# Moving the differential values ahead of the inverse's corner products in a fused two-block transformer kernel

## The chip, the cores and the metric

The kernel runs on one core of a Trainium2 chip. The metric is the time of one execution on the device in microseconds (us). Each core has five engines with queues of their own: TensorE (PE, matrix products), VectorE (DVE), ScalarE (ACT), GpSimd (POOL) and SyncE (SP, which here issues the loads of weights). An engine takes its instructions in the order of its queue; an instruction whose input is late holds up everything behind it.

## The reference

Two transformer blocks on 512 tokens of width 1024, all in float32. The first block (two layers with attention and a gated feed-forward) is untouched here. In the second block the input goes through one projection into two mixers: an RWKV-7 recurrence with 8 heads of 64, and a differential attention with 4 heads:

```python
def step(state, inp):                      # RWKV-7, per token
    sa = einsum('bhvk,bhk->bhv', state, -kk_t)
    state = state * w_t + sa x (kk_t * a_t) + v_t x k_t      # outer products
    return state, einsum('bhvk,bhk->bhv', state, r_t)
...
attn = softmax(q1 k1) - lam * softmax(q2 k2)    # differential attention
out = einsum('bhqk,bhkv->bhqv', attn, vh)
```

Both outputs are normed, joined and multiplied with w_out; a convolutional feed-forward follows.

## The kernel before

Everything is kept transposed (features on partitions, 512 tokens along the free axis). A product in float32 accuracy is made of three passes: a weight chunk of 128x1024 is loaded by SP into `raw` (three buffers), ACT casts it to `whi` (L178), DVE or POOL subtracts to get the rest, `wlo` (L179), and PE adds hi*hi, hi*lo and lo*hi. `whi` and `wlo` have two buffers each, so the cast of a chunk waits until PE is through with the chunk before the last.

The recurrence is computed in chunks of 64 tokens (8 chunks `c`). Inside a chunk it needs the inverse of a triangular matrix for every head. `within` makes these matrices on PE (`pslm`, masked by DVE into `lms`) and copies their 32x32 blocks into `G`; `inverse32` inverts all blocks on DVE alone (tiles Lb, Xb, Pb, Qb, L1685 to L1707), in one long chain that ends with the transposed results `tN` and `tT`. Two sets of small PE products, the corner products `psi` (L1476, 32x32 pieces, from `tN`) and `psi2` (L1482, from `tT`; the trace calls both tiles psi), build the 64x64 inverses in `TT`. Then the chunk loop runs (L1487 to L1526): per chunk the products pxy, pu, pst and the state `S2`.

The differential attention needs its queries and keys (`diff_qk`, i = 0 to 7, tile psd) and its values (`diff_v`, two halves of two weight chunks; 96 matrix products of 256 columns each, tile psdv, L1317, copied to `dv` by ACT, L1322). `work` is the generator of its 16 query blocks: a step is a pair of scores (PE z, DVE L680, ACT L682), a turn (`t`, L698) or a product with the values (`o`, L706); it has 50 steps. `fill(n)` runs n steps of a generator between the products of the recurrence.

The order around the change: two blocks set the order of PE by hand (`manual_schedule` for PE). The first ends with `diff_qk(4..7)` and `diff_v(0)`, the second begins with the corner products. The second half of the values, `values1 = diff_v(1)`, is a generator with 8 pieces of 12 products; VF = (3, 2, 2, 2) spreads it: three pieces between `psi` and `psi2`, two after `chunk_in(0)`, two inside chunk 0, the last in `rest()`. Only then may `work` begin, as it uses the xl tiles as scratch. The later fills are FILLS = (2, 2, 1, 6, 6, ...): 2, 2 and 1 steps per chunk, and 6 and 6 in `tail`, which is placed by the planner. The other engines' queues are ordered by the planner, a simulation with costs of its own: it puts first what it expects to be ready first. `zero` (L1385, POOL) shares its buffer with `Qb` of the inverse. The copies from tT to TT go to DVE (L1463) and ACT (L1464). SLOTS says which part of the recurrence runs where between the `diff_qk`.

Of the kernel before, what the change touches and what calls it, by code (L numbers as in the profile page):

```python
# [12 lines left out]
ALU = mybir.AluOpType  # L13
# [13 lines left out]
def f(t):  # L27
    return t.bitcast(F32)
# [54 lines left out]
class Net:  # L83
# [88 lines left out]
    def chunk(self, ap, eng=None, raw=None, parts=None):  # L172
        nc, n = self.nc, ap.shape[-1]
        if raw is None:
            raw = self.wp.tile([128, 1024], F32, tag="raw", name="raw", bufs=3)
            nc.sync.dma_start(out=raw[:, :n], in_=ap)
        hi, lo = parts or [self.wp.tile([128, 1024], F32R, tag=n_, name=n_, bufs=2) for n_ in ("whi", "wlo")]
        nc.scalar.copy(out=hi[:, :n], in_=raw[:, :n])  # L178
        (eng or nc.vector).tensor_sub(out=lo[:, :n], in0=raw[:, :n], in1=f(hi[:, :n]))  # L179
        return hi, lo  # L180

# [930 lines left out]
    def block2_attn(self):  # L1112
        nc, A = self.nc, self.A
        v_, g_, s_, t_ = nc.vector, nc.gpsimd, nc.scalar, nc.tensor
        with ExitStack() as st:
# [224 lines left out]
            with self.tc.manual_schedule(engines={mybir.EngineType.PE}):  # L1340
# [3 lines left out]
                for ks in (range(7), (7,)):  # L1344
                    for ps, (hi, lo) in zip(first, ws):
                        for k in ks:
                            c = slice(k * 128, k * 128 + 128)
# [25 lines left out]
                X, tN, tT = self.inverse32(pp, G)  # L1373
                dv = pp.tile([128, 4, 512], F32, tag="dv", name="dv")
                for i in range(4, 8):
                    diff_qk(i, g_)
                list(diff_v(0))
            values1 = diff_v(1)
# [3 lines left out]
            xs2, uv2, bv2, y2 = [pp.tile([128, 1056], F32, tag=f"bk{i}", name=n_)[:, 0:1024].rearrange("p (a b) -> p a b", a=2) for i, n_ in enumerate(("xs", "uv", "bv", "yy"))]  # L1382
            yv = lambda t, c: t[:, c % 2, :].rearrange("p (h v) -> p h v", v=64)
            zero = pp.tile([128, S], F32R, tag="zq", name="zero")
            g_.tensor_scalar(out=zero.rearrange("p (a b) -> p a b", a=4), in0=self.ident.unsqueeze(1).to_broadcast([128, 4, 128]),  # L1385
                             scalar1=0.0, scalar2=None, op0=ALU.mult)
            dist2 = [pp.tile([128, S], F32, tag="smask", name="dist"), None]
            nc.sync.dma_start(out=dist2[0], in_=A["dist"])
            S2, yr = [], []
# [2 lines left out]
            def rest():  # L1392
                for _ in values1:
                    pass
                dist2[1] = self.xp.tile([128, S], F32, tag="xh2", name="dist2")
                yr.extend(self.xp.tile([128, S], F32, tag=f"xh{4 + t}", name=f"yr{t}") for t in range(4))
                for i in range(2):
                    S2.append(self.xp.tile([128, 4, 2, 64], F32, tag=f"xh{i}", name=f"S{i}"))
                    g_.memset(S2[i], 0.0)
# [13 lines left out]
            fill = lambda n, of=work: [next(of, None) for _ in range(n)]  # L1413
# [33 lines left out]
            def tail():  # L1447
                chunk_out(7)
                fill(FILLS[3])
                norm_out(2)  # L1450
                fill(FILLS[4])
                norm_out(3)
                fill(1000)

            with self.tc.manual_schedule(engines={mybir.EngineType.PE}):

                TT = [pp.tile([128, 4, 2, 64], F32, tag=n_, name="TT") for n_ in ("pb0", "pb1", "e20", "e21")]
                pm = pp.tile([128, 4, 8, 32], F32, tag="bk2", name="pm")
                half = [(64 - 64 * par, slice(64 - 64 * par, 96 - 64 * par), slice(96 - 64 * par, 128 - 64 * par)) for par in range(2)]
                for t in range(4):  # L1460
                    for _, lo, hi in half:
                        g_.memset(TT[t][hi, :, :, 0:32], 0.0)
                        v_.tensor_copy(out=TT[t][lo, :, :, 0:32], in_=tT[lo, :, 2 * t:2 * t + 2, :])  # L1463
                        s_.copy(out=TT[t][hi, :, :, 32:64], in_=tT[hi, :, 2 * t:2 * t + 2, :])  # L1464

                def corner(ps, hh, rows, mm, out):
                    for par in range(2):
                        for cp in range(4):
                            for h in range(4):
                                mm(ps[half[par][rows], cp, h, :], par, cp, 4 * hh + h)  # L1470
                    for par in range(2):
                        out(par, ps[half[par][rows]])

                for hh in range(2):
                    ps = ((pg, pv)[hh]).tile([128, 4, 4, 32], F32, tag="go"[hh], name="psi")
                    corner(ps, hh, 2, lambda o, par, cp, h: t_.matmul(o, lm(par, cp, h)[half[par][1], half[par][0] + 32:half[par][0] + 64],  # L1476
                                                                      tN[half[par][1], cp, h, :], start=True, stop=True),
                           lambda par, p: (s_.copy if par else v_.tensor_copy)(out=pm[half[par][2], :, 4 * hh:4 * hh + 4, :], in_=p))
                fill(VF[0], values1)
                for hh in range(2):  # L1480
                    ps = pc.tile([128, 4, 4, 32], F32, tag="c", name="psi2")
                    corner(ps, hh, 1, lambda o, par, cp, h: t_.matmul(o, pm[half[par][2], cp, h, :], tT[half[par][2], cp, h, :], start=True, stop=True),  # L1482
                           lambda par, p: [(s_.copy if par else v_.tensor_copy)(out=TT[2 * hh + i][half[par][1], :, :, 32:64], in_=p[:, :, 2 * i:2 * i + 2, :])
                                           for i in range(2)])
                chunk_in(0)
                fill(VF[1], values1)
                for c in range(8):  # L1487
                    cp, par = c // 2, c % 2
                    U = E[1 - par]
                    b, uv, xs = banks[c], uv2[:, c % 2, :], xs2[:, c % 2, :]  # L1490
                    if c:
                        for t in range(4):
                            t_.matmul(b[:, t * 128:t * 128 + 128], ar[t][:, c, :], S2[c % 2][:, t].rearrange("p e v -> p (e v)"),
                                      start=False, stop=True, skip_group_check=True)
                    v_.tensor_copy(out=xs[U, 0:256], in_=b[U, 0:256])
                    v_.tensor_copy(out=xs[U, 256:512], in_=b[U, 256:512])
                    if c:
                        chunk_out(c - 1)
                    fill(FILLS[0]) if c else fill(VF[2], values1)
                    for g in range(2):  # L1500
                        pu = pc.tile([128, 256], F32, tag="c", name="pu")
                        for h in range(4 * g, 4 * g + 4):
                            t_.matmul(pu[U, hs[h - 4 * g]], TT[h // 2][U, cp, h % 2, :], xs[U, hs[h]], start=True, stop=True)
                        (s_.copy if g else v_.tensor_copy)(out=uv[U, 256 * g:256 * g + 256], in_=pu[U])
                    if c:
                        fill(FILLS[1])
                    else:
                        rest()
                        fill(VF[3])
                    if c < 7:  # L1510
                        ps = pc.tile([128, 4, 64], F32, tag="c", name="pst")
                        for h in range(8):
                            t_.matmul(ps[E[h % 2], h // 2, :], bkt[:, c, hs[h]], uv[:, hs[h]], start=True, stop=True)
                        for e in range(2):
                            new = S2[(c + 1) % 2][E[e], :, e, :]
                            if c == 0:
                                v_.tensor_copy(out=new, in_=ps[E[e]])
                            else:
                                old = S2[c % 2][E[e], :, e, :]
                                g_.tensor_tensor(out=new, in0=old, in1=dcs[E[e], :, c:c + 1].to_broadcast([64, 4, 64]), op=ALU.mult)  # L1520
                                v_.tensor_tensor(out=new, in0=new, in1=ps[E[e]], op=ALU.add)
                    if c < 7:
                        chunk_in(c + 1)
                    fill(FILLS[2])
                    if c in (4, 6):
                        norm_out(c // 2 - 2)  # L1526
                if TAIL[0] == 0:
                    tail()
# [320 lines left out]
FILLS = (0, 2, 2, 4, 6)  # L1849
# [139 lines left out]
def constants():  # L1989
# [37 lines left out]
VF = (3, 2, 2, 2)  # L2027
# [18 lines left out]
FILLS = (2, 2, 1, 6, 6, 0, 0)  # L2046
# [2 lines left out]

SLOTS = [["", "", "", "", "decays", "norm1 next keep:01"],  # L2050
         ["late keep:2", "turn:v keep:3", "keep:4", "within:0 within:1 norm1 keep:5", "turn:bh bonus keep:6", "turn:kh within:2 within:3 next keep:7"],
         ["late", "turn:v", "", "within:0 within:1", "within:2 within:3 bonus", "turn:bh turn:kh"]]
CUT = (5, 5)
NEWT = 1
FAST = (0, 0, 0, 1)
# [24 lines left out]
```

## Time and profile before

| | us |
|---|---|
| median of 3 runs | 2021.73 (2016.67 to 2022.11) |
| profiled execution, its own time | 2025.36 |
| span in that profile (first to last instruction) | 2023.6 |
| PE busy | 1934.1 (96%) |
| DVE busy | 1348.1 (67%) |
| ACT busy | 892.2 (44%) |
| POOL busy | 420.5 (21%) |

Busy times are of the whole span. Matrix products are pipelined, so the duration of one is longer than the distance to the next. PEclk is the granted clock of TensorE, as a share of 2.4 GHz; 0.50 is its lower level, 1.2 GHz. The stretch that the change touches runs from 1408 to about 1590 us of the span.

### The profile page before, as it was taken

The page shows a single profiled execution, that of the slowest core. Times are in us where ns is not written, and L with a number is a line of the kernel's source. Part 1 is how long each engine was busy: PE and PEld are TensorE (multiplying, and loading weights), DVE is VectorE, ACT ScalarE, POOL GpSimd, SP SyncE. Part 2 cuts the span into 40 slices and gives each one's busy share as a digit, 9 for nine tenths or more (in the row PEclk, how much of TensorE's full clock was granted, in tenths as well). Part 3 has the DMA queues.
Part 4 walks back from the last instruction along what each step waited for, and adds up shares of the span by engine and source line. Part 5 has one row for each costly group of instructions (what it writes and reads, how often), then busy time and mean ns, then how long its engine had stood idle before and what let it go on. Part 6 is the DMA issues. An engine that isn't in the chain of part 4 may idle for free.

```text
span 2023.6 us, 29687 instructions
## 1 busy us (share of the span) xinstructions
PE 1934.1 (96%) x11652; PEld 1655.3 (82%) x11652; DVE 1348.1 (67%) x2295; ACT 892.2 (44%) x1530; POOL 420.5 (21%) x429
## 2 busy tenths in 40 slices
PE   9999998999999999988999999899899999999997
PEld 8766788999997877778899998678687788888886
DVE  6555568777777576557868676777948568666424
ACT  5454444444444555444434344544245445444321
POOL 3434210000002175320000001344333242111001
PEclk9998998999999999999999999999989999999999
DMA  4210142423223210123423232322111113232332
GB/s 162 99 58 7 32 155 84 138 71 118 88 82 100 74 49 23 32 81 121 142 77 111 87 107 61 111 97 69 63 43 34 63 55 103 95 103 94 95 95 71
DMA packets 58124, 169.58 MB, mean 84 GB/s; under 512 B 6304, under 2 KB 13504, under 8 KB 57984
## 3 DMA queue, kind: packets, MB, share of 16 engines
q1 hardware_dynamic: 54672, 162.70, 24.5%
q10 hardware_dynamic: 3232, 4.72, 0.7%
q8 instruction: 92, 1.51, 0.3%
q14 instruction: 48, 0.39, 0.1%
q0 software_dynamic: 80, 0.26, 0.1%
HBM read 161.89 MB, written 5.77 MB: 83 GB/s over the span
## 4 chain that ended last, share of the span: by engine, by line
PE 80%; DVE 13%; ACT 3%; issue 2%; DMA 1%; POOL 1%; SPq 0%; DVEq 0%; ACTq 0%; POOLq 0%
PE pa L733 8%; PE o L185 7%; PE o L184 6%; PE o L186 6%; PE pb L733 5%; PE p L733 4%; PE pd L186 4%; PE pd L184 4%; PE pd L185 4%; PE po L706 2%; PE t L698 1%; DVE l L217 1%; PE psq L184 1%; PE psq L185 1%; PE psq L186 1%
## 5 line engine op out<-in xcount | busy, mean ns | idle before, releaser
L178 ACT CAST whi<-raw 128x1024 fp32r<-128x1024 f32 (+3 forms) x146 | 144.5, 992 | 273.3 <-PE o L185 91.0
L179 DVE TENSOR_TENSOR wlo<-raw,whi 128x1024 fp32r<-128x1024 f32 (+3 forms) x138 | 164.1, 1190 | 123.0 <-ACT whi L178 122.7
L733 PE MATMUL pa<-t,h 128*128 128x256 f32 x960 | 177.7, 286 | 10.1 <-DVE u L910 8.4
L1044 POOL TENSOR_TENSOR acc<-acc,sqt 128x256 f32<-128x256 f32 (+1 forms) x58 | 70.8, 1220 | 489.7 <-ACT sqt L1043 488.2
L217 DVE TENSOR_TENSOR l<-r,h 128x1024 fp32r<-128x1024 f32 x104 | 127.1, 1222 | 56.1 <-ACT h L216 55.8
L733 PEld LDWEIGHTS pa<-t,h 128*128 128x128 f32 x960 | 152.5, 194 | 12.1 <-ACT ah L861 8.7
L733 PE MATMUL pa<-t,l 128*128 128x256 f32 x480 | 137.5, 286 | 2.2 <-DVE l L217 2.2
L216 ACT CAST h<-r 128x1024 fp32r<-128x1024 f32 x104 | 107.9, 1046 | 65.2 <-PE pd L185 19.9
L185 PE MATMUL o<-xl,whi 128*128 128x512 f32 (+1 forms) x352 | 134.6, 382 | 2.1 <-DVE xl L224 2.1
L184 PE MATMUL o<-xh,whi 128*128 128x512 f32 (+1 forms) x352 | 134.8, 383 | 0.0
L186 PE MATMUL o<-xh,wlo 128*128 128x512 f32 (+1 forms) x352 | 134.0, 381 | 0.0
L186 PE MATMUL pd<-ah,l 128*128 128x512 f32 x320 | 125.6, 392 | 1.9 <-DVE l L217 1.9
L184 PE MATMUL pd<-ah,h 128*128 128x512 f32 x320 | 125.6, 392 | 0.3 <-ACT h L216 0.3
L185 PE MATMUL pd<-al,h 128*128 128x512 f32 x320 | 125.3, 391 | 0.0
L733 PE MATMUL p<-t,h 128*128 128x256 f32 x640 | 116.8, 283 | 4.2 <-ACT h L216 4.2
L733 PE MATMUL pb<-t,h 128*128 128x256 f32 x640 | 116.5, 282 | 0.0
L733 PEld LDWEIGHTS p<-t,h 128*128 128x128 f32 x640 | 99.9, 190 | 5.9 <-ACT h L216 4.6
L733 PEld LDWEIGHTS pb<-t,h 128*128 128x128 f32 x640 | 99.9, 191 | 0.9
L216 ACT CAST h<-raw 128x768 fp32r<-128x768 f32 (+2 forms) x76 | 62.4, 821 | 82.3 <-PE pd L185 58.8
L733 PEld LDWEIGHTS pa<-t,l 128*128 128x128 f32 x480 | 93.1, 194 | 3.0 <-DVE l L217 3.0
L733 PE MATMUL p<-t,l 128*128 128x256 f32 x320 | 90.6, 283 | 3.0 <-DVE l L217 3.0
L733 PE MATMUL pb<-t,l 128*128 128x256 f32 x320 | 90.6, 283 | 1.0 <-DVE l L217 1.0
(550 smaller groups left out, 5338.1 us busy)
## 6 DMA issues: line engine op xcount, KB each, us to landing
r<-w_gu SPq DMA_DIRECT2D x88, 512.0 KB, 3.5
raw<-w_gu SPq DMA_DIRECT2D x56, 512.0 KB, 3.4
raw<-w_dn SPq DMA_DIRECT2D x48, 384.0 KB, 4.1
raw<-w_in SPq DMA_DIRECT2D x22, 512.0 KB, 3.4
raw<-w_dn SPq DMA_DIRECT2D x16, 448.0 KB, 3.2
raw<-w_qka SPq DMA_DIRECT2D x8, 512.0 KB, 3.5
raw<-w_dn SPq DMA_DIRECT2D x16, 256.0 KB, 2.6
raw<-w_out SPq DMA_DIRECT2D x8, 512.0 KB, 3.4
```

Of the source, the lines that this page charges most:

```text
L178: nc.scalar.copy(out=hi[:, :n], in_=raw[:, :n])
L179: (eng or nc.vector).tensor_sub(out=lo[:, :n], in0=raw[:, :n], in1=f(hi[:, :n]))
L184: mm(out, lh, rh, start=start, stop=False)
L185: mm(out, lh, rl, start=False, stop=False)
L186: return mm(out, ll, rh, start=False, stop=stop)
L216: self.nc.scalar.copy(out=hi, in_=src)
L217: (eng or self.nc.vector).tensor_sub(out=lo, in0=src, in1=f(hi))
L698: nc.tensor.transpose(t[:, c], s[:, c], self.ident)
L706: nc.tensor.matmul(po[:, b * 128:b * 128 + 128], v(kb), w[:, kb * 128:kb * 128 + 128], start=kb == 0, stop=kb == b)
L733: self.nc.tensor.matmul(c, l, r, start=first and n == 0, stop=k == 3 and n == 2, skip_group_check=True)
L1044: return nc.gpsimd.tensor_add(out=self.acc[:, c], in0=self.acc[:, c], in1=t)
```

## The change

All pieces of `values1` are now run by `rest()` at the head of the second block, ahead of the corner products; `zero` is made after that and pinned behind what is already traced on POOL; the ACT copies into TT are put behind the last weight cast of the values in ACT's queue. The places that were filled with pieces of `values1` are filled with as many steps of `work`. In SLOTS, the last two `within` move up beside the first two, ahead of the first half of `diff_qk(2)` instead of into its middle.

```diff
-        nc.scalar.copy(out=hi[:, :n], in_=raw[:, :n])
+        self.cast = nc.scalar.copy(out=hi[:, :n], in_=raw[:, :n]).ins
...
-            g_.tensor_scalar(out=zero.rearrange("p (a b) -> p a b", a=4), in0=self.ident.unsqueeze(1).to_broadcast([128, 4, 128]),
-                             scalar1=0.0, scalar2=None, op0=ALU.mult)
...
-                for t in range(4):
-                    for _, lo, hi in half:
-                        g_.memset(TT[t][hi, :, :, 0:32], 0.0)
-                        v_.tensor_copy(out=TT[t][lo, :, :, 0:32], in_=tT[lo, :, 2 * t:2 * t + 2, :])
-                        s_.copy(out=TT[t][hi, :, :, 32:64], in_=tT[hi, :, 2 * t:2 * t + 2, :])
+                rest()
+
+                self.tc.keep_in_program_order(g_.tensor_scalar(
+                    out=zero.rearrange("p (a b) -> p a b", a=4), in0=self.ident.unsqueeze(1).to_broadcast([128, 4, 128]),
+                    scalar1=0.0, scalar2=None, op0=ALU.mult))
+                with self.tc.issue_after(self.cast):
+                    for t in range(4):
+                        for _, lo, hi in half:
+                            ... (the same three)
...
-                fill(VF[0], values1)
+                fill(VF[0])
...
-                fill(VF[1], values1)
+                fill(VF[1])
...
-                    fill(FILLS[0]) if c else fill(VF[2], values1)
+                    fill(FILLS[0]) if c else fill(VF[2])
...
-                        rest()
                         fill(VF[3])
...
-         ["late", "turn:v", "", "within:0 within:1", "within:2 within:3 bonus", "turn:bh turn:kh"]]
+         ["late", "turn:v", "", "within:0 within:1 within:2 within:3", "bonus", "turn:bh turn:kh"]]
```

## Rows read from the trace of the kernel before

**Rows 1.** The page: busy time of PE and DVE; the chain that ended last.
```profile
PE 1934.1 (96%) x11652; PEld 1655.3 (82%) x11652; DVE 1348.1 (67%) x2295; ACT 892.2 (44%) x1530; POOL 420.5 (21%) x429
...
PE 80%; DVE 13%; ACT 3%; issue 2%; DMA 1%; POOL 1%; SPq 0%; DVEq 0%; ACTq 0%; POOLq 0%
```

**Rows 2.** PE's waits, 1440 to 1600: total us, times, longest.
```profile
PE psi L1476 <- DVE tN L1706: 9.9, 1, 9.9
PE pu L1503 <- DVE xs L1495: 1.6, 1, 1.6
```

**Rows 3.** Windows: length, busy us (instructions) of each engine, granted clock, DMA.
```profile
1446.20:1452.20 6.00, 6.00 (x50) 5.79 (x48) 5.83 (x10) 1.05 (x1) 0.00 (x0) 1.00 0.22 81
1452.20:1462.40 10.20, 0.29 (x4) 0.08 (x2) 9.99 (x10) 0.00 (x0) 3.67 (x2) 0.75 0.00 0
1462.40:1467.40 5.00, 5.00 (x50) 4.94 (x51) 4.02 (x9) 3.13 (x8) 0.15 (x1) 0.50 0.29 105
1467.40:1474.30 6.90, 6.90 (x126) 6.77 (x125) 0.70 (x1) 5.34 (x10) 3.21 (x2) 0.99 0.24 78
1474.30:1477.70 3.40, 3.40 (x19) 3.36 (x17) 0.70 (x1) 0.58 (x1) 2.07 (x2) 0.51 0.21 60
1477.70:1484.20 6.50, 6.50 (x150) 6.34 (x149) 0.76 (x2) 0.62 (x2) 2.02 (x2) 0.99 0.14 52
1484.20:1491.40 7.20, 7.20 (x43) 6.83 (x40) 2.30 (x5) 1.67 (x3) 2.04 (x2) 0.53 0.01 2
...
1497.40:1556.00 58.60, 57.60 (x624) 45.99 (x623) 50.40 (x184) 34.91 (x93) 22.12 (x24) 1.00 0.03 11
1556.00:1562.90 6.90, 4.62 (x50) 3.82 (x49) 6.76 (x31) 2.50 (x6) 0.00 (x0) 1.00 0.20 61
1562.90:1587.20 24.30, 22.50 (x128) 17.26 (x127) 16.51 (x62) 14.17 (x35) 4.80 (x4) 0.79 0.33 113
```

**Rows 4.** Timeline of POOL: start, length, instruction, idle before it and its releaser.
```profile
1425.57 2.39 POOL L179 TENSOR_TENSOR wlo<-raw,whi 128x1024 fp32r<-128x1024 f32 x1 [3.92 <-ACT whi L178]
...
1458.73 1.49 POOL L1385 TENSOR_SCALAR zero<-ident 128x512 fp32r<-128x512 f32 x1 [13.78 <-DVE Pb L1701]
1460.18 2.37 POOL L179 TENSOR_TENSOR wlo<-raw,whi 128x1024 fp32r<-128x1024 f32 x1
```

**Rows 5.** Timeline of ACT: TT copies, a weight cast, the copies of the first values.
```profile
1464.19 3.30 ACT L1464 COPY TT<-tT 32x256 f32<-32x256 f32 x8 [16.94 <-DVE tT L1707]
1467.51 1.05 ACT L178 CAST whi<-raw 128x1024 fp32r<-128x1024 f32 x1
...
1470.91 1.57 ACT L1322 ACTIVATE dv<-psdv,rsy 128x256 f32<-128x256 f32 x4 [1.21 <-PE psdv L1317]
```

**Rows 6.** Timeline of SP: the four loads of the value weights.
```profile
1427.99 17.32 SPq L176 DMA_DIRECT2D raw<-w_dv  x4
```

**Rows 7.** Timeline of DVE: masks of `within`, and pieces of the inverse.
```profile
1410.97 0.68 DVE L1286 TENSOR_TENSOR lms<-pslm,lmask 128x512 f32<-128x512 f32 x1
1414.39 0.69 DVE L1286 TENSOR_TENSOR lms<-pslm,lmask 128x512 f32<-128x512 f32 x1 [2.73 <-PE pslm L1283]
...
1425.75 2.54 DVE L1689 TENSOR_TENSOR Pb<-Xb,Lb 128x162 f32<-128x162 f32 x1
...
1428.68 0.54 DVE L1689 TENSOR_TENSOR Pb<-Xb,Lb 128x200 f32<-128x200 f32 x1
...
1456.74 1.90 DVE L1701 TENSOR_TENSOR Pb<-Qb,Xb 128x1024 f32<-128x1024 f32 x1
...
1462.19 1.96 DVE L1707 STREAM_TRANSPOSE tT<-Xb 128x1024 f32<-128x1024 f32 x1
```

**Rows 8.** Timeline of PE: the first product after the stall; two steps of work.
```profile
1462.39 1.94 PE L1476 MATMUL psi<-tN,lms 32*32 32x32 f32 x36 [9.91 <-DVE tN L1706]
...
1568.58 1.06 PE L706 MATMUL o<-w,dv 128*128 128x128 f32 x8
1569.56 1.13 PE L679 MATMUL z<-dqk,dqk 64*128 64x512 f32 x4
```

More of the change, by code (lines that the diff above doesn't have):

```diff
@@ L1459, in block2_attn @@
                 half = [(64 - 64 * par, slice(64 - 64 * par, 96 - 64 * par), slice(96 - 64 * par, 128 - 64 * par)) for par in range(2)]
-                for t in range(4):
-                    for _, lo, hi in half:
-                        g_.memset(TT[t][hi, :, :, 0:32], 0.0)
-                        v_.tensor_copy(out=TT[t][lo, :, :, 0:32], in_=tT[lo, :, 2 * t:2 * t + 2, :])
-                        s_.copy(out=TT[t][hi, :, :, 32:64], in_=tT[hi, :, 2 * t:2 * t + 2, :])
+                rest()
[5 more added lines that the diff above has]
+                        for _, lo, hi in half:
+                            g_.memset(TT[t][hi, :, :, 0:32], 0.0)
+                            v_.tensor_copy(out=TT[t][lo, :, :, 0:32], in_=tT[lo, :, 2 * t:2 * t + 2, :])
+                            s_.copy(out=TT[t][hi, :, :, 32:64], in_=tT[hi, :, 2 * t:2 * t + 2, :])
                 def corner(ps, hh, rows, mm, out):
```

## The prediction

> **What bounds the kernel now.** I read the page's busy times first, then the chain that ended last: PE is busy 96% of the span and carries 80% of that chain [rows 1], so a change pays only where PE waits or runs at its lower clock. PE's waits in the stretch of the change are next: one of 9.9 us stands out, the first `psi` waiting for `tN` of the inverse; the next longest in the list is 1.6 us [rows 2]. The windows then give each part of the stretch, and the reader should see two kinds of loss there [rows 3]. From 1452.2 to 1462.4 PE is busy 0.29 of 10.2 us: 9.9 us idle. And in three windows it is busy all the time at a granted clock of about 0.50, which is 1.2 GHz: 5.0 us at 0.50, 3.4 at 0.51, 7.2 at 0.53. Work done there would have taken half the time at 2.4 GHz; length times (1 - clock) gives 2.5 + 1.7 + 3.4 us, and 0.1 from the two windows at 0.99 between: 7.7 us. Together the old order loses 17.6 us between 1452 and 1492.
>
> Why PE idles is read on POOL and ACT. The second weight chunk of the first values needs its `wlo` from POOL. POOL holds `zero` first, which waits 13.78 us for the buffer of `Qb`, that is for DVE's last L1701; `wlo` starts at 1460.18 [rows 4], though its cast, the one ACT instruction (1.05 us) of the window from 1446.2, was over by 1447.3 [rows 3]. So values that have nothing to do with the inverse wait for it. ACT repeats the pattern one step later: the TT copies wait 16.94 us for `tT`, and the cast of the third chunk stands behind them until 1467.51, though its buffer was free when the first chunk was used up at 1452.2 [rows 3, 5].
>
> **The change part by part.** *Values ahead, `zero` pinned behind, TT copies behind the last cast.* The first chunk's 48 products run as before to 1452.2, 0.12 us each (50 in 6.0 us [rows 3]). The second `wlo` follows its cast at 1447.3 and takes 2.4 us [rows 4]; at 1449.7 it is there before PE asks. PE goes on to 1452.2 + 5.8 = 1458.0. The third chunk: cast at 1452.2, 1.05 us [rows 5], `wlo` to 1455.8, asked for at 1458.0. All four loads were issued by 1445.3 [rows 6] and move past nothing. One new wait: half of the second psdv pair is in a single PSUM bank, free only when ACT has copied the first values, 1.57 us after 1458.0 [rows 5]; six products (0.7 us) go ahead of it, and with the hand-overs I take 1.1 us (0.9 to 1.6). What stands behind on PE is the rest of the values, nothing else. The fourth chunk: cast after those copies to 1460.7, `wlo` to 1463.1, asked for at 1464.9. PE ends the values at 1446.2 + 23.0 + 1.1 = 1470.3. On POOL the memsets of S2 and `zero` (1.49 us [rows 4]) come after 1463.1 and are first wanted by the chunk products behind `psi` and `psi2`, some 10 us later; that work hides them. The 9.9 us go whole.
>
> *What is late next.* The inverse must be done by 1470.3. It ended with `tT` at 1464.15 [rows 7]. Three POOL subtractions now fall into it. The trace shows what one does: a Pb product of 162 elements takes 2.54 us while POOL's `wlo` runs, one of 200 elements 0.54 alone [rows 4, 7], so 2.0 us each, 6.0 in all.
>
> *`within` together.* The third mask of `within` came at 1414.39; now it can follow the second at 1411.65 [rows 7], so the inverse starts 2.7 us earlier. PE's work there is the same and only in another order: nothing on PE. `tT` is then at 1464.15 + 6.0 - 2.7 = 1467.5 and `tN` 2 us before, 4.8 us ahead of PE. That is the cover; if it failed by x us, PE would idle x. The TT copies (3.30 us on ACT [rows 5]) end at 1470.8, before anything needs TT.
>
> *Steps of `work` in place of pieces of values.* Seven steps move from the end of the stage to here; PE has the same work in sum. But the pieces of values were good cover: 128-row products with no waits. A score step waits for DVE to empty two PSUM banks. I count three places with new waits: the three scores between `psi` and `psi2`, the copies xs ahead of pu, the copies uv ahead of pst. The loop's own mix of the same steps leaves 1.0 us idle in 58.6 [rows 3], the lower end (near zero a place); the pu wait of 1.6 us [rows 2] at each place, 4.8, the upper. I take 3.0 us, nearer to the upper end, as here scores follow each other directly.
>
> *Clock.* With the values, the dense work between the corner products is gone. In the old order the clock fell once PE had run `psi` (6.9 us at 0.99, then 3.4 at 0.51) and again after `psi2` (6.5 at 0.99, then 7.2 at 0.53) [rows 3], each time without idle. Those two cost 5.1 us. The fall at 1462.4, after the stall, disappears with it. Now the two sets stand near each other and `psi2` may itself run at 1.2 GHz: at worst one unbroken stretch from 1474 to about 1493, 19 us, 9.5 lost. At best none, since the chunk loop's mix of the same steps holds 1.00 for 58.6 us. I take 7 us, midway between 5.1 and 9.5, because what lies between is scores, not dense products.
>
> The Trainium skill, "TensorE: Matmul & The Clock Gate", section "HAM oscillation — how this bites in real kernels", puts it as a matter of gaps: PE loses its clock when it sits idle too long. By that rule the new order, without long gaps, would keep 2.4 GHz, a rival below. The trace speaks against it: PE was busy 6.90 of 6.90 us before the fall to 0.51 [rows 3].
>
> *The tail.* The steps 39 to 45 of `work` leave it: one pair of scores at 1.13 us and some 20 passes of 128 columns at 0.13 (8 in 1.06) [rows 8], about 4 us of PE. From 1556 to 1587.2 PE loses 2.3 + 1.8 us idle and 0.21 of 24.3 = 5.1 us by the clock [rows 3], while the norm of the last chunk goes its way over DVE, POOL and ACT. With fewer scores DVE serves that chain sooner. Ends: 4 us worse, if the chain is as long and PE merely idles, to 4.6 better, if half of the 9.2 lost there goes; I take 1.5 better, a little to the better side of the middle, as DVE is shown busy 16.5 of 24.3 us there.
>
> **Sum.** Gone: 9.9 + 7.7 = 17.6. New: 1.1 + 3.0 + 7.0 = 11.1. Tail: 1.5 better. Gain 8.0 us. The profiled execution took 2025.36 us, 3.6 above the median of the runs; all terms are differences within one stage, so I take them from the median: 2021.73 - 8.0 = 2013.7. What this kernel's measurement can tell from no change is about 0.3%, 6.1 us: the border of faster is 2015.7.
>
> **The rivals.**
> *The clock holds*: no clock loss, 7 us more gain, 2006.7. For it: the loop's mix at 1.00. Against: the two falls without idle. 0.12. It is what the Trainium skill's rule on gaps would lead to.
> *The tail gives it back*: the end of the stage hangs on the last chunk's chain, and the 4 us of steps that filled PE there are missing. Tail 4.0 worse instead of 1.5 better: gain 2.5, 2019.2. For it: PE is idle and half-clocked there already. Against: the products with w_out fill in, and the chain itself waits behind score work on DVE. 0.18.
> *The queue trap moves*: the planner, which expects the inverse early, puts another instruction that waits for the inverse ahead of one that PE needs (the copies of the first values behind the TT copies, say). PE then waits from 1458.7 to about 1467.5 again, 8.8 us, and the change doesn't do what it says: 2022.5. Against: the pins name the two traps seen. 0.09.
> *Slower: the clock stays down in the chunk loop.* Place: PE after `psi`. With no dense product left, the clock that falls at about 1474 isn't given back by the 64-row work. Without clock loss the gain is 15.0 us, so from 30 us at 1.2 GHz on, that is from about 1504, the change loses; to the end of the loop at 1540 it would be 66 us, 33 lost, 18 us slower: 2039.7. For it: the longest stretch at 0.53 was the one with the most small products in it. Against: the loop held 1.00 throughout. 0.06.
> The forecast has 0.55; its own range is 2010 to 2017.5.
>
> **Chances.** Faster by over 0.3%: 0.78 of the forecast (0.43), all of the held clock (0.12), 0.02 of the tail's: 0.57. Slower by over 0.3%: the clock rival 0.06, and 0.03 of the queue trap with other bad placements by the planner: 0.09. Same: the rest, 0.34. The range goes from the held clock to the tail's case and the queue trap's edge, 2006 to 2021; left out is most of the slower case and half the trap.
>
> **What would show it.** In the new profile: `zero` behind the last `wlo` of the values on POOL; 192 psdv products in one row at about 0.12 us with one gap near 1 us, ended by 1470 to 1471; `psi` starting without waiting for `tN`; a DVE chain whose tT ends near 1467; a clock of 0.5 from about 1474 for some 14 us; the chunk loop at 1.00 again; a tail with fewer scores and an earlier last norm. Wrong would be: a wait of `psi` for `tN` of several us (the cover was too thin), a copy or cast on ACT behind TT copies, a clock of 0.5 beyond 1500, or a tail in which PE idles more than the 4.1 us of before.

## The result: slower by 0.5%, and the profile after

The changed kernel takes 2029.7 us (2027.16 to 2032.29), the kernel before 2021.26 us beside it: a ratio of 1.0051, 95% interval 1.0038 to 1.0064. Forecast were 2013.7 us. The page after, busy times and chain, against [rows 1]:

```profile
PE 1937.0 (95%) x11652; PEld 1655.5 (82%) x11652; DVE 1350.9 (67%) x2295; ACT 893.0 (44%) x1530; POOL 419.4 (21%) x429
...
PE 82%; DVE 10%; issue 3%; ACT 3%; DMA 1%; POOL 1%; SPq 0%; DVEq 0%; ACTq 0%; POOLq 0%
```

DVE's share of the chain fell from 13% to 10%, PE's grew from 80% to 82%. Next PE's waits from 1380 to 1620, where [rows 2] had `psi` waiting 9.9 us for `tN`:

```profile
PE psdv L1317 <- ACT whi L178: 10.3, 1, 10.3
PE z L679 <- DVE smst L680: 2.3, 2, 1.9
PE psdv L1317 <- POOL wlo L179: 1.8, 1, 1.8
```

`psi` no longer waits. The values do: 10.3 us for a cast and 1.8 us for the subtraction behind it. ACT shows who held that cast (start, length, instruction, idle before it and its releaser):

```profile
1443.01 1.05 ACT L178 CAST whi<-raw 128x1024 fp32r<-128x1024 f32 x1 [4.39 <-PE psd L185]
1462.78 1.24 ACT L1422 COPY uv<-vt 64x512 f32<-64x512 f32 x2 [18.72 <-DVE tT L1710]
1464.04 1.05 ACT L178 CAST whi<-raw 128x1024 fp32r<-128x1024 f32 x1
1465.12 1.57 ACT L1322 ACTIVATE dv<-psdv,rsy 128x256 f32<-128x256 f32 x4
...
1467.64 3.30 ACT L1468 COPY TT<-tT 32x256 f32<-32x256 f32 x8
```

The TT copies stand behind the last cast, as the change asks. But the two `uv` copies that `chunk_in` issues (L1422) now stand ahead of the third value cast. They write the tile with tag bk1, which the inverse's `Xb` holds until `tT` has read it, so ACT sits idle for 18.72 us. In the kernel before, the same copies came behind that cast, which started at 1467.51 [rows 5]:

```profile
1468.46 1.24 ACT L1424 COPY uv<-vt 64x512 f32<-64x512 f32 x2
```

POOL shows the planned half of the change at work, against [rows 4]: the second `wlo` at 1444.13 follows its cast at once, and `zero` is last:

```profile
1444.13 2.40 POOL L179 TENSOR_TENSOR wlo<-raw,whi 128x1024 fp32r<-128x1024 f32 x1 [2.40 <-ACT whi L178]
1465.17 2.35 POOL L179 TENSOR_TENSOR wlo<-raw,whi 128x1024 fp32r<-128x1024 f32 x1 [18.63 <-ACT whi L178]
...
1473.45 1.50 POOL L1460 TENSOR_SCALAR zero<-ident 128x512 fp32r<-128x512 f32 x1
```

The windows after (columns as in [rows 3]; the first figure after the five engines is the granted clock):

```profile
1442.99:1454.72 11.73, 11.73 (x97) 11.52 (x95) 11.42 (x14) 1.05 (x1) 2.40 (x1) 1.00 0.25 86
1454.72:1467.60 12.88, 0.78 (x4) 0.32 (x2) 10.21 (x14) 4.76 (x8) 2.35 (x1) 0.62 0.00 0
1467.60:1471.30 3.70, 3.70 (x17) 3.70 (x18) 0.00 (x0) 3.23 (x9) 1.16 (x2) 0.50 0.41 142
1471.30:1480.83 9.53, 9.53 (x81) 9.40 (x79) 1.23 (x1) 1.66 (x3) 5.11 (x4) 1.00 0.36 112
1480.83:1485.00 4.17, 4.17 (x133) 4.12 (x132) 0.90 (x2) 2.46 (x5) 0.00 (x0) 1.00 0.02 4
1485.00:1515.60 30.60, 28.34 (x252) 21.92 (x248) 15.20 (x51) 8.46 (x28) 4.76 (x5) 0.50 0.06 18
...
1536.30:1556.00 19.70, 18.70 (x202) 15.02 (x200) 17.36 (x63) 11.89 (x30) 6.98 (x8) 1.00 0.01 2
1556.00:1590.00 34.00, 31.89 (x308) 26.30 (x307) 30.65 (x113) 20.28 (x48) 8.66 (x8) 1.00 0.28 94
```

Two losses show. From 1454.7 to 1467.6 PE is busy 0.78 us: idle as before, for another instruction. And from 1485.0 to 1515.6, after `psi`, it is busy 28.34 of 30.60 us at 0.50, 1.2 GHz; nothing of this length stands in [rows 3]. PE's own timeline shows it in one pair, `psi` and `psi2`, 128 products of 32x32 each in the trace, 3.93 us at 1.00 and 6.47 us at 0.50:

```profile
1480.83 3.93 PE L1480 MATMUL psi<-tN,lms 32*32 32x32 f32 x128
...
1487.14 1.43 PE L679 MATMUL z<-dqk,dqk 64*128 64x256 f32 x4 [1.95 <-DVE smst L680]
...
1491.13 6.47 PE L1486 MATMUL psi<-tT,pm 32*32 32x32 f32 x128
```

To compare kernels I count, over windows of 1 us from 1440 to 1600, PE's idle time (length less busy) and what the clock takes (busy time x (1 - granted clock)). Before: 15.0 idle + 12.5 clock = 27.5 us. After: 18.7 + 19.8 = 38.5. That is 11.0 us more, beside 10.3 us by the ratio. The count takes the clock's loss at its highest: of the 6.47 us of `psi2` it calls 3.2 lost, and the pair above shows 2.5.

### The profile page after: what moved, and what is told of

It is laid out like the page before. It is cut to its first block, busy times and chain, and to the rows that moved or that the text cites. A ratio compares the mean times of both kernels' runs of the same rounds, so it can differ in the third digit from the quotient of the medians.

```text
span 2030.4 us, 29687 instructions
## 1 busy us (share of the span) xinstructions
PE 1937.0 (95%) x11652; PEld 1655.5 (82%) x11652; DVE 1350.9 (67%) x2295; ACT 893.0 (44%) x1530; POOL 419.4 (21%) x429
## 4 chain that ended last, share of the span: by engine, by line
PE 82%; DVE 10%; issue 3%; ACT 3%; DMA 1%; POOL 1%; SPq 0%; DVEq 0%; ACTq 0%; POOLq 0%
PE pa L733 8%; PE o L185 6%; PE o L186 6%; PE o L184 6%; PE pb L733 5%; PE p L733 4%; PE pd L186 4%; PE pd L184 4%; PE pd L185 4%; PE po L706 2%; PE t L698 1%; DVE l L217 1%; PE psq L184 1%; PE psr L184 1%; PE psq L185 1%
## 5 line engine op out<-in xcount | busy, mean ns | idle before, releaser
L733 PE MATMUL pa<-t,h 128*128 128x256 f32 x960 | 177.6, 286 | 10.3 <-DVE u L910 8.4
```

The costliest lines, as they stand in the source:

```text
L733: self.nc.tensor.matmul(c, l, r, start=first and n == 0, stop=k == 3 and n == 2, skip_group_check=True)
```

## Experiments

Theory 1: the queue trap moved to the `uv` copies. Theory 2: with the dense value products gone from between `psi`, `psi2` and chunk 0, the clock falls and stays low, idle or not.

**The uv copies behind the last value cast** (uv_pinned).

```
+                last_cast.append(self.cast)          # behind rest()
...
-                s_.copy(out=uv2[V, c % 2, :], in_=vt[V, cp, :])
+                with self.tc.issue_after(last_cast[0]):
+                    s_.copy(out=uv2[V, c % 2, :], in_=vt[V, cp, :])
```

> The changed kernel with one thing more: the two `uv` copies that `chunk_in` issues on ScalarE (line 1422, the first waits for the inverse's last transpose) are held behind the last cast of the differential values' weights, as the copies of TT already are; nothing else differs. Theory 1 (the trap went to another instruction): these copies, planned ahead of the third value cast, hold it and with it the 64 products of the second half. The waits of 10.3 + 1.8 us go, and the 3.7 us of products at half clock behind them run at full clock (1.9 us): 2029.7 - 14.0 = 2015.7 us. Theory 2 (no dense products left behind psi): a second loss of some 15 us stays, seen as a granted clock of 0.50 for about 30 us while psi2, z, t, o and the first chunk run. Rival A: that half clock is a consequence of the idle 12 us before; then it goes with the stall, and the time is near 2001 us. Rival B: something else holds the third cast (its transfer, a free buffer): the time stays at 2029 to 2030 us and the wait keeps its size under another name.

Measured 2016.58 us (2011.01 to 2018.69), 0.9982 of before (0.9974 to 0.9991). ACT now, with the third value cast at 1447.25, released by PE, the fourth at 1453.69, and the copies behind all casts of the values:

```profile
1447.25 1.05 ACT L178 CAST whi<-raw 128x1024 fp32r<-128x1024 f32 x1 [5.13 <-PE psdv L1317]
...
1453.69 1.05 ACT L178 CAST whi<-raw 128x1024 fp32r<-128x1024 f32 x1
1463.07 3.31 ACT L1471 COPY TT<-tT 32x256 f32<-32x256 f32 x8 [8.33 <-DVE tT L1713]
1466.39 1.25 ACT L1424 COPY uv<-vt 64x512 f32<-64x512 f32 x2
```

Its windows, the values and `psi` first:

```profile
1441.60:1465.36 23.76, 23.28 (x190) 22.59 (x188) 23.25 (x26) 6.30 (x13) 12.89 (x7) 1.00 0.25 84
1465.36:1469.30 3.94, 3.93 (x129) 3.82 (x128) 0.64 (x2) 3.87 (x8) 0.00 (x0) 1.00 0.01 4
1469.30:1489.50 20.20, 17.82 (x167) 12.70 (x168) 11.12 (x34) 7.91 (x23) 2.04 (x2) 0.50 0.16 53
...
1489.50:1513.10 23.60, 21.61 (x240) 17.18 (x241) 15.26 (x52) 11.61 (x32) 8.72 (x10) 0.99 0.01 2
1513.10:1520.30 7.20, 7.20 (x46) 6.55 (x44) 4.26 (x21) 2.60 (x7) 1.56 (x3) 0.55 0.01 2
```

The stall is gone with one pin: theory 1 holds, rival B falls. Rival A falls too: PE was busy 27.2 of 27.7 us when the clock fell at 1469.3, right behind `psi`, and it stayed at 0.50 for 20.2 us. Here the half clock came without a long idle time before it. The Trainium skill ("TensorE: Matmul & The Clock Gate", section "HAM oscillation — how this bites in real kernels") ties the loss to idle gaps; this trace doesn't agree: the 27.7 us before the fall hold 0.5 us of idle time in all.

**`zero` alone pinned, values where they were** (zero_pin_alone).

```
-            g_.tensor_scalar(out=zero..., scalar1=0.0, scalar2=None, op0=ALU.mult)
+            self.tc.keep_in_program_order(g_.tensor_scalar(out=zero..., scalar1=0.0, scalar2=None, op0=ALU.mult))
```

> The kernel before with one edit: `zero` on GpSimd (line 1385) keeps its place in program order, behind the first two wlo of the differential values, so that it cannot be planned ahead of the second wlo; the four pieces of the values stay between the inverse's products as they were. Theory 2 (the dense value products between psi, psi2 and the first chunk keep TensorE's clock up): the wait of 9.9 us goes and no new half clock comes: 2021.3 - 9.9 = 2011.4 us, down to 2003.7 if the half clock before psi goes as well. Rival: the planner finds another instruction to put ahead (a copy that waits for the inverse ahead of a cast), and the wait stays at 9 to 12 us under another name: 2020 to 2024 us.

Measured 2013.38 us (2010.15 to 2015.26), 0.9964 (0.9951 to 0.9977). One added call gives nearly the time that was forecast for the whole change, but not in the way expected: the wait shrinks from 9.9 to 6.2 us only. Counted from the start of `Lb`, PE asks for `psi` 5.6 us later, as it now runs the other 47 products of the first values ahead of it, and `tN` comes 1.9 us later, with one more subtraction beside the inverse:

```profile
PE psi L1477 <- DVE tN L1707: 6.2, 1, 6.2
```

The clock is at 0.50 for the 12.9 us that begin with `psi`, this time behind idle time, and at 0.53 for 3.3 us behind `psi2`. With value pieces in between, it is then 1.00 up to 1556:

```profile
1461.40:1474.30 12.90, 11.12 (x149) 10.85 (x149) 5.29 (x11) 8.95 (x18) 5.18 (x3) 0.50 0.14 42
1474.30:1481.70 7.40, 7.40 (x162) 6.99 (x160) 1.52 (x4) 1.20 (x4) 3.32 (x4) 0.96 0.25 75
1481.70:1485.00 3.30, 3.30 (x18) 3.18 (x17) 0.77 (x2) 0.17 (x2) 0.74 (x1) 0.53 0.00 0
1485.00:1556.00 71.00, 68.36 (x724) 55.69 (x724) 57.53 (x212) 39.39 (x101) 22.11 (x24) 1.00 0.06 17
```

**Values dealt out again, all casts up front** (split_4211), on top of uv_pinned.

```
+                cs = [self.chunk(A["w_dv"][2 * half + c], g_) for c in range(2)] if half else None
...
-                    hi, lo = self.chunk(A["w_dv"][2 * half + c], g_)
+                    hi, lo = cs[c] if half else self.chunk(A["w_dv"][c], g_)
...
-                rest()
+                fill(4, values1)     # ahead of psi
...
-                fill(VF[0])
+                fill(2, values1)     # between psi and psi2
...
-                fill(VF[1])
+                fill(1, values1)     # behind chunk_in(0)
...
+                        rest()       # in chunk 0
                         fill(VF[3])
```

> The kernel of uv_pinned with the eight value pieces dealt out again, behind their casts: four ahead of psi, two between psi and psi2, one behind the first chunk_in and the last inside chunk 0, whose work steps then follow it; all casts are issued before any copy that waits for the inverse. Theory 1 and 2 together: no wait for a cast, and the clock between psi and chunk 1 is 1.00 or falls for less than 15 us: 2029.7 - 14.0 - 10 to 15 = 2000.7 to 2005.7 us. Theory 1 alone (the half clock has nothing to do with where the value products stand): as uv_pinned, near 2015.7 us. Rival A (half clock follows the idle time): as uv_pinned too, both near 2001 us.

Measured 2007.1 us (1997.22 to 2009.71), 0.9927 (0.9909 to 0.9945): the lowest median of the study, and 1.4 us above the range expected. It differs from uv_pinned by where four of the eight pieces stand (both casts of this half come ahead of `psi`, as they do there), and 1.2 GHz shrinks from 20.2 + 7.2 us up to 1556 to 6.4 + 3.2 us:

```profile
1457.40:1461.50 4.10, 2.35 (x75) 2.35 (x75) 4.05 (x4) 0.52 (x2) 3.67 (x4) 0.95 0.41 128
1461.50:1467.90 6.40, 6.40 (x75) 6.34 (x73) 3.68 (x10) 5.55 (x11) 0.00 (x0) 0.50 0.01 3
1467.90:1474.90 7.00, 7.00 (x158) 6.52 (x158) 2.68 (x7) 1.83 (x5) 1.87 (x2) 0.99 0.26 77
1474.90:1478.10 3.20, 3.20 (x22) 2.98 (x22) 0.37 (x2) 0.00 (x0) 0.17 (x1) 0.50 0.00 0
1478.10:1556.00 77.90, 75.14 (x770) 60.03 (x768) 67.86 (x244) 48.16 (x124) 26.72 (x27) 1.00 0.15 49
```

By this alone the order of other work could be the reason as well. Hence the next two.

**Zero products behind psi and psi2** (dense).

```
+                banks[0] = pr.tile([128, 512], F32, tag="r", name="pxy")
+                for _ in range(12):    # once behind psi, once behind psi2
+                    t_.matmul(banks[0], zero[:, 0:128], zero, start=True, stop=False, skip_group_check=True)
```

> The kernel of uv_pinned with work added that changes no value: 24 zero products of 128x512, twelve right behind psi and twelve right behind psi2, into the bank that chunk 0 clears with such a product anyway. At 0.23 us each (two psdv products of 256 columns at 0.12 us) they cost 5.6 us at full clock. Theory 2 (it is the want of dense products behind psi that brings 0.50, and no idle time is needed for it): the 19.6 us at 0.50 behind psi shrink to 8 us or less, which gives back 5.8 us or more: 2012 to 2017 us, against 2016.6 without them. Rival (0.50 comes on its own course, or after the waits of 1.5 us and less in this stretch): the half clock keeps its 20 us, the products cost 5.6 us or, in part at 0.50, up to 8: 2022 to 2025 us.

Measured 2013.17 us (2009.96 to 2015.01), 0.9964 (0.9948 to 0.9980). With 24 products more that change nothing, the kernel is 3.4 us faster than uv_pinned by the medians, 3.6 by the ratios (each run has its own measurement of the kernel before beside it). The two intervals overlap a little, so what is safe is that 5.5 us of added work (24 products at 0.23 us) cost nothing that shows. The single 0.50 of 20.2 us becomes two parts, 0.63 over 4.6 us and 0.55 over 7.2 us:

```profile
1471.40:1476.00 4.60, 4.60 (x14) 3.38 (x16) 3.16 (x4) 2.83 (x6) 0.00 (x0) 0.63 0.49 127
1476.00:1481.20 5.20, 4.50 (x82) 3.25 (x83) 3.90 (x20) 3.28 (x12) 0.00 (x0) 1.00 0.25 94
1481.20:1488.40 7.20, 7.20 (x78) 6.17 (x72) 2.16 (x6) 1.25 (x4) 2.04 (x2) 0.55 0.00 0
```

**The control: small products in place of the zero products** (light): `psi`'s own products again, 64 calls behind `psi` and 64 behind `psi2`, into the same bank.

```
+                t_.matmul(banks[0].rearrange(...)[half[par][2], cp, h, :], lm(par, cp, h)[...],
+                          tN[half[par][1], cp, h, :], start=True, stop=True, skip_group_check=True)
```

> The control for the zero products: the kernel of uv_pinned with psi's own 128 products of 32x32 computed a second time into the same unused bank, half of them right behind psi and half right behind psi2, so TensorE is as busy as with the zero products (3.9 us at full clock, 6.5 us at 0.50 by psi and psi2 in uv_pinned), but not with dense ones. Theory 2: the 0.50 behind psi stays 20 us or grows by the products' length; 2016.6 + 6.5 = 2023 us, up to 2026. Rival (busy time of any kind keeps the clock up): it shrinks as with the zero products, and the time is 2014 to 2020 us.

Measured 2026.17 us (2020.9 to 2029.33), 1.0028 (1.0016 to 1.0039): 9.6 us slower than uv_pinned by the medians, 9.3 by the ratios, intervals far apart. The control is twice as large as I expected: a call is two products in the trace, so 128 calls add 256, from 11652 in uv_pinned to 11908 here, and at the 3.93 us of `psi`'s 128 that is 7.9 us at full clock, not 3.9.

```profile
PE 1941.6 (96%) x11908; PEld 1660.3 (82%) x11908; DVE 1351.8 (67%) x2295; ACT 893.2 (44%) x1530; POOL 420.8 (21%) x429
...
1464.40:1470.00 5.60, 5.60 (x198) 5.60 (x198) 2.27 (x4) 5.53 (x11) 0.00 (x0) 1.00 0.04 7
1470.00:1497.80 27.80, 27.10 (x373) 22.01 (x369) 9.70 (x34) 6.90 (x22) 2.04 (x2) 0.51 0.13 39
```

PE is busy 27.10 of 27.80 us and holds 0.51 throughout, with more work added than in dense. Being busy with 32x32 products doesn't bring 2.4 GHz back, and zeros in 128x512 do: theory 2 holds. The wait of 1.5 us for `pm` behind `psi` in uv_pinned is gone in both kernels, so it isn't what sets them apart. The mean granted clock of every run says the same, not of the profiled ones alone: 0.975 to 0.979 in dense, 0.971 to 0.976 in uv_pinned, 0.967 to 0.974 in light. The two kinds of products differ in rows and in columns at once; which of the two counts was not tried.

**The old slots** (old_slots): the changed kernel with the line of SLOTS of before.

> The changed kernel with the slots of the kernel before for the last four chunk products (two of them in the fourth slot, two in the fifth). Theory: these slots move the inverse by at most 0.5 us, as the two traces show at Lb, and the loss lies behind it: 2029.2 to 2031 us, the same as the changed kernel. Rival: putting the four together cost part of the 8.4 us (the fourth mask waits 2.66 us, and the clock gate falls earlier): 2022 to 2027 us.

Measured 2030.52 us (2027.28 to 2032.61), 1.0052 (1.0040 to 1.0065): the same as the changed kernel. The four `within` together neither cost nor give anything there. **The same in split_4211** (split_4211_slots):

> split_4211 with the slots of the kernel before for the last four chunk products. With TensorE waiting 1.8 us for the inverse there, a start of the inverse that is 0.5 us later costs at most that: 2007.1 to 2007.6 us, the same. Rival: the four together cost something that the stall hid before: 2002 to 2006 us.

Measured 2007.24 us (2005.17 to 2013.29), 0.9938 (0.9918 to 0.9958), again no difference.

**Five pieces ahead of psi** (split_5210):

```
-                fill(4, values1)
+                fill(5, values1)
```

> As split_4211, with five value pieces ahead of psi, two between psi and psi2, one behind the first chunk_in and none in chunk 0. The fifth piece (12 products for each of four row groups less, some 1.5 us) fills the 1.8 us in which TensorE waits for tN there. Theories 1 and 2: the wait goes (1.8 us), the 6 us at 0.50 that begin with it go too (3 us); chunk 0 has one dense piece less, so some of that may come back later: 2007.1 - 2 to 5 = 2002 to 2005 us, and 2007 if it all comes back. Rival (the small pieces in chunk 0 cover its own waits): 2008 to 2011 us.

Measured 2008.45 us (2003.99 to 2010.97), 0.9936 (0.9917 to 0.9954); not told apart from split_4211, and in the range of the rival. The 1.8 us before `psi` are gone, but `psi2` waits 2.5 us for DVE's `pm` copies, which stand behind the `wlo` of a w_out chunk, whose cast stands on ACT behind the TT and uv copies:

```profile
1464.61 1.05 ACT L178 CAST whi<-raw 128x1024 fp32r<-128x1024 f32 x1
```

```profile
1465.69 1.23 DVE L179 TENSOR_TENSOR wlo<-raw,whi 128x1024 fp32r<-128x1024 f32 x1 [3.31 <-ACT whi L178]
1466.94 1.31 DVE L1486 COPY pm<-psi 32x512 f32<-32x512 f32 x2
```

My expectation did not have this further trap of the kind. Behind this wait the clock falls within `psi2` and stays at 0.50 from 1470.0 to 1489.5, with PE busy 19.11 of 19.50 us, though the value piece behind `chunk_in(0)` stands in that stretch: one piece did not bring it back.

The count of idle and clock from 1440 to 1600, beside the times (the last column is (ratio - 1) x 2021.3):

| kernel | idle us | clock us | sum | ratio to before | us |
|---|---|---|---|---|---|
| before | 15.0 | 12.5 | 27.5 | 1 | |
| after | 18.7 | 19.8 | 38.5 | 1.0051 | +10.3 |
| uv_pinned | 8.3 | 14.2 | 22.5 | 0.9982 | -3.6 |
| zero_pin_alone | 12.8 | 7.5 | 20.3 | 0.9964 | -7.3 |
| old_slots | 19.7 | 16.2 | 35.9 | 1.0052 | +10.5 |
| split_4211 | 6.2 | 5.1 | 11.3 | 0.9927 | -14.8 |
| split_4211_slots | 6.2 | 5.1 | 11.3 | 0.9938 | -12.5 |
| split_5210 | 7.4 | 10.0 | 17.4 | 0.9936 | -12.9 |
| dense | 5.4 | 8.6 | 14.0 | 0.9964 | -7.3 |
| light | 6.6 | 18.4 | 25.0 | 1.0028 | +5.7 |

Against the 27.5 of before, the sums of the seven kernels without added work give +11.0, -5.0, -7.2, +8.4, -16.2, -16.2 and -10.1: within 4 us of the measured times. Each count is of one profiled execution, and these lie up to 5.2 us off their medians (split_4211 took 2001.92, before 2025.36), so no closer agreement can be asked of them. The added work goes on top: dense -13.5 + 5.5 = -8.0, near its -7.3; light -2.5 + 7.9 = +5.4, near its +5.7.

## Why the prediction was wrong

*The step that failed* is the clearing of the queue traps: "the pins name the two traps seen", and with it "The third chunk: cast at 1452.2" and the 1.1 us put down for all new waits of the values. The cast came at 1464.04, and the values waited 12.1 us. A third instruction waiting for the inverse, the `uv` copies, took the place on ACT that the TT copies had left. The prediction had this as a rival at 0.09, with the right mechanism and the wrong instruction, and priced the wait at 8.8 us. Its time of 2022.5 us was 7 us short: 3.3 us by the wait itself, and the rest, as far as the count goes, by the clock. With that step made good (uv_pinned) the gain was 3.6 us by the ratio where 8.0 were forecast. That it came so near is partly luck, as a larger loss of clock and a better tail stand against each other.

*The clock* was mis-sized. Forecast 7.0 us, at worst 9.5. In uv_pinned the half clock behind `psi` cost 17.82 x 0.50 = 8.9 us and a second one in the chunk loop 7.2 x 0.45 = 3.2; after the change the first was 28.34 x 0.50 = 14.2. I had ended it at `psi2`, but in the changed kernel `psi2`, the scores and the first chunks ran in it for 30.6 us before it ended. The loop's 1.00 in [rows 3] showed that this mix kept a full clock it was given; I read it as if the mix would soon restore one. In uv_pinned it did not always keep one either: 0.99 for 23.6 us, then 0.55 for 7.2. The slower rival named this place with 0.06, for 30 us or more at 1.2 GHz; that is the length in the changed kernel, but there the trap was half of the loss.

*The stall*: "the 9.9 us go whole" holds for `psi`'s wait. That they are worth 9.9 is not so: in zero_pin_alone, where the trap of `zero` alone is taken away, 6.2 us of waiting for the inverse come back. My reading of the stall was incomplete as well: in PE's queue 36 of the `psi` products stood ahead of the other 47 value products, so PE waited for `tN`, as [rows 8] shows. The late `wlo` ended at 1462.55, 0.16 us after `psi` began; the pin on `zero` frees the values because the order of PE changes with it.

*The inverse*: I counted 6.0 us longer from three subtractions on POOL. From Lb's start to tT's end it is 47.5 us before and 51.5 us in uv_pinned, 4.0 longer. The gain of 2.7 us from `within` together did not come: Lb starts 2.4 us after the start of the `bon` products before and 2.3 us in uv_pinned. The fourth mask follows those products in every order; with the other three early it only waits longer. In the changed kernel:

```profile
1412.18 0.69 DVE L1286 TENSOR_TENSOR lms<-pslm,lmask 128x512 f32<-128x512 f32 x1 [2.66 <-PE pbon L1265]
```

I took the third mask for the last. The two errors of 2.0 and 2.6 us nearly cancel: the cover was 4.3 us (tN ends at 1461.0, `psi` asks at 1465.4), forecast 4.8.

*The small terms* were right or nearly so. Bank and cast hand-overs 0.5 us in uv_pinned (0.2 for dv, 0.3 for a wlo), forecast 1.1. Waits for pm, smst and uv came to 3.1 us (1.5, 0.7, 0.9), where 3.0 were forecast for three places, partly others; two waits of the next chunks for the state `S`, 1.1 and 1.0 us, were not in the list. The tail was better than the 1.5 us forecast: from 1556 on, idle and clock were 9.2 us by [rows 3] and are 2.5 + 31.55 x 0.05 = 4.0 in uv_pinned. By how much of this the tail itself ends sooner was not measured apart.

## What to carry to other kernels

When an instruction that waits for a late result is moved back in an in-order queue, list every other instruction of that queue that waits for the same result, also by a shared buffer: pinning the two that the trace shows lets the planner put a third in their place. Don't gather all dense products ahead of a run of small ones: the same work can be worth more between them, here 9.5 us by the medians for dealing four pieces of values out again, most of it clock (14.2 to 5.1 us in the count). To tell an effect of the clock from one of order, add dense products that change nothing, and small ones as a control.

## Unexpected

The granted clock fell to 0.50 with PE busy 27.2 of the 27.7 us before (uv_pinned), and it stayed at 0.51 over 27.10 busy us of 27.80 (light). Adding 24 zero products did not cost the 5.5 us they take, and adding 256 small ones of 7.9 us cost 9.6. And the runs of one kernel lie up to 13 us apart (before, beside dense: 2014.77 to 2027.82).
